# Norm factors of the second token half multiplied into its input blocks, and the query and output-operand splits moved to other turns, in a one-core attention layer

## The chip, the core and the metric

The kernel runs on one core of one Trainium2 chip. The metric is the device time of one execution in microseconds (us). The engines are named as the profile names them: PE (TensorE; its weight loads stand apart as PEld), DVE (VectorE), ACT (ScalarE), POOL (GpSimd) and SP (SyncE, whose queue issues nearly all DMAs here). Every engine works through its own instructions in order; tiles written by one and read by another are guarded by semaphores, so an instruction that waits holds up all that stand behind it on its engine.

## The reference

One encoder layer on x of 2048 tokens by 1024 channels, tokens lying on a grid of 32 rows by 64 columns:

```
h = rmsnorm(x, norm_0)                         # x * rsqrt(mean(x*x)) * norm_0
q, k, v, gate = split(h @ w_in_0, 4)           # w_in_0: 1024 x 4096; 16 heads of 64
o = neighbourhood_attention(q, k, v, rpb_0)    # each token sees a window of 8 rows x 16 columns,
                                               # with a learned bias, softmax in float32
x = x + (o * silu(gate)) @ w_out_0
return rmsnorm(x, norm_f)
```

The norm has two factors: `norm_0`, one per channel, and 1/rms, one per token. `h @ w` can take the second either before the product (in h) or after it (on the result's tokens), since a factor per token passes through the product. The change is about that choice.

## The kernel before, in words

**Precision.** Matrix products are made of three products of split operands: each operand t is split into a high part h (ACT copies it into the fp32r type) and the rest l = t - h (DVE subtracts), and PE adds h·h, h·l and l·h. A split therefore costs one ACT and one DVE instruction of 128x512.

**Layout.** Inputs stand transposed, channels on partitions and 512 tokens to a block; c = 0, 1, 2, 3 numbers the blocks of tokens. Tokens 0 to 1023 (c = 0, 1) are the first half, the rest (c = 2, 3) the second.

**Stage one** (`stage_one`, to 326 us): for the first half, the values v of all heads (`values_of`), and then q, k and gate with Strassen-Winograd's seven products instead of eight (`seven_products`): a unit is one kind (k, q, g) of one pair of heads j, 12 units in all, 7 x 12 matmuls each. After each product DVE adds the bank to an earlier one (`add`, `out_`, L432, L438), and where a result is complete it is multiplied by `rb[c]`, the tokens' 1/rms spread over all partitions: by POOL (L439) or, for product 2, by DVE out of PSUM (`evac`, L326 and L328). `give` then splits a k, or makes SiLU of a gate (ACT tanh L340, DVE L341), and a DMA stores it 12 matmuls later.

**The norm.** `stats` makes 1/rms from sums of squares, `diagonal` puts it on a diagonal and splits that, and `spread_rstd` lets PE multiply it with ones, so that ACT can copy `rb[c]` out of a bank. Only `norm_0` is applied to inputs: `split_to` and `split_x` scale by `g0` while they split (L498, L499, L155, L156). Values take 1/rms as ACT's scale when they leave PSUM (`evac_v`, L377).

**Stage two** (`stage_two`, 326 to 471 us): the same for the second half with one pair of heads j = 0 (three units of seven products) and all values. The other heads' q, k, gate of the second half (`projections`) are 36 plain groups of 24 matmuls (L365 to L369), which fill PE's time between attention turns.

**Attention** (the last loop, 471 to 1043 us): 64 turns, two for each pair of heads and block of 8 grid rows; a turn has two column blocks. Turn i is one iteration: `begin` issues loads and, on even turns, POOL's tables of bias plus mask (`bias`, L945, up to six additions `em`); `feed` puts about 22 matmuls of projections, later of the output projection (`outputs`, L1223 to L1227), on PE; `middle` splits the queries (`split_q`, L498 and L499, tiles `qh`, `ql`); then comes PE's attention block: transposes of turn i-2's weights (`turns`, L986, copied out by DVE L1011 and ACT L1010 as `pta`), scores of turn i (`scores`, L963, then L970 on DVE and the exponential L973 on ACT), and values of turn i-2 (`values`, L1031, tile `o`). `normalise` has POOL scale the weights (L981) by DVE's reciprocal (L979). All of it takes turns in eight PSUM banks handed out in order: a bank is used again eight allocations later, when its readers are done.

**The order** of instructions is fixed by hand. A clock counts filling matmuls; `store` puts DMAs and other late work into a list with a lag on that clock; `feed` keeps at least 8 matmuls between the last split or evacuation and the attention block. Output operands are split by `split_og` (ACT L1103, DVE L1104, two halves) when `ahead` in `outputs` finds the next one loaded 28 matmuls ago. Loads of keys (L896), queries (L900), values (L920) and gates (L927) are issued by SP in the order of the list; `later_loads` spaces them.

Of the kernel before, what the change touches and what calls it, by code (L numbers as in the profile page):

```python
# [70 lines left out]
def build(ctx, tc, x, xr, xt, wg, rpb, w_out, n0, nf, masks, out):  # L71
# [65 lines left out]
    rb = {}  # L137
# [14 lines left out]
    def split_x(a, b, t, tiles=None):  # L152
        h, l = tiles or (xs([128, 512], F32R, "hh"), xs([128, 512], F32R, "hl"))
        hh[a, b], hl[a, b] = h, l
        nc.scalar.activation(h, t, AF.Copy, scale=g0[:, a:a + 1])  # L155
        nc.vector.scalar_tensor_tensor(l, t, g0[:, a:a + 1], h.bitcast(F32), op0=OP.mult, op1=OP.subtract)  # L156

    def use_item(it):
# [3 lines left out]
        if kind == "x":  # L162
            split_x(a, b, t, (hh[a, b], hl[a, b]))
# [125 lines left out]
    pending = []  # L289
# [23 lines left out]
    def flush(c):  # L313
        if c not in rb:
            if c not in dgs:
                diagonal(c)
            spread_rstd(c)
        for e in [e for e in pending if e[0] == c]:
            pending.remove(e)
            e[1]()  # L320

    def evac(kind, hp, c, p, then=None):
        state["event"] = clock[0]
        tmp = ev([128, 512], F32, "tmp")
        if kind == "k":
            nc.vector.tensor_tensor(tmp, p, rb[c], OP.mult)  # L326
        else:
            nc.vector.tensor_tensor(blocked(tmp), tiled(p), tiled(rb[c]), OP.mult)  # L328
# [5 lines left out]
    def give(kind, hp, c, tmp):  # L334
        while sum(e[1][0] in "kqg" for e in later) > 1:
            later.pop(0)[2]()
        s = slice(c * 512, c * 512 + 512)
        if kind == "g":
            sg = ev([128, 512], F32, "sg")
            nc.scalar.activation(sg, tmp, AF.Tanh, scale=0.5)  # L340
            nc.vector.scalar_tensor_tensor(sg, sg, 1.0, tmp, op0=OP.add, op1=OP.mult)  # L341
            written.add(("g", hp, c))
            store(("g", hp, c), 12, lambda: nc.sync.dma_start(sgd[hp][:, s], sg))
            return
        written.add((kind, hp, c))
        if kind == "q":
            store(("q", hp, c), 12, lambda: nc.sync.dma_start(qd[hp][:, s], tmp))
            return
        hi = ev([128, 512], F32R, "hi")
        lo = ev([128, 512], F32R, "lo")  # L350
        nc.scalar.activation(hi, tmp, AF.Copy)
        nc.vector.tensor_tensor(lo, tmp, hi.bitcast(F32), OP.subtract)
# [22 lines left out]
    def evac_v(u, t, p):  # L375
        v = ev([128, 512], F32, "v")
        nc.scalar.activation(v, p, AF.Copy, scale=rt[:, t:t + 1])  # L377
# [10 lines left out]
    def seven_products(us, c0, X1, also):  # L388
# [45 lines left out]
        def out_(n, a, c, P, u, then):  # L434
            kind, j = us[n]
            tmp = ev([128, 512], F32, "tmp")
            lay, of = (lambda t: t, lambda t: t) if kind == "k" else (blocked, tiled)
            nc.vector.tensor_tensor(lay(tmp), of(B[n, P]), of(u), OP.add)  # L438
            nc.gpsimd.tensor_tensor(lay(tmp), lay(tmp), of(rb[c]), OP.mult)  # L439
# [16 lines left out]
        def run():  # L456
            then = []
            for i, (n, P) in enumerate(seq):
# [7 lines left out]
                elif P == 2:  # L466
                    evac(kind, 2 * j, c0, B[n, 2], then)
# [74 lines left out]
    def stage_one():  # L542
# [31 lines left out]
        def also(n, i):  # L574
# [10 lines left out]
            if (n, i) == (-1, 3):  # L585
                spot2 = mkp([128, 3, 512], F32, "spot")
                L2["x11"] = [spot2[:, k] for k in range(3)] + [lp([128, 512], F32, "land")]
                for k in range(4):
                    load_x(2, "x11", k, L2["x11"][k])
            if n == 0:  # L590
                if i == 0:
# [3 lines left out]
                    for k in (0, 1):  # L595
                        split_to(*X2["B11"][k], L2["x11"][k], gain("x11", k))
                elif i == 1:
                    L2["x21"] = [p([128, 512], F32, "land") for p in (mp, mp, ep, ep)]
                    for k in range(4):
                        load_x(2, "x21", k, L2["x21"][k])  # L600
                    for a, b in ((1, 1), (0, 2), (1, 2)):
                        load_v0(0, a, b)
                    for k in (2, 3):
                        split_to(*X2["B11"][k], L2["x11"][k], gain("x11", k))
# [12 lines left out]
                elif i in (4, 5):  # L617
                    for k in (0, 1) if i == 4 else (2, 3):
                        split_to(*X2["B21"][k], L2["x21"][k], gain("x21", k))
# [3 lines left out]

        ahead, run = seven_products(us, 0, X1, also)
# [113 lines left out]
    def stage_two():  # L738
        x12, x11, x21 = L2["x12"], L2["x11"], L2["x21"]
        x22 = [qp([128, 512], F32, "land") for _ in range(4)]  # L740
        for k in range(4):
# [3 lines left out]
                 "T4": [(vp, 512)] * 4 + [(mp, 512)] * 2 + [(ep, 512), (qp, 512)]}  # L745
# [49 lines left out]
        def t123(*ks):  # L795
            def g():
                for k in ks:
                    y = ev([128, 512], F32, "y")
                    a, b, c = x11[k], x12[k], x22[k]
                    nc.scalar.activation(y, b, AF.Copy, scale=gain("x12", k))  # L800
                    nc.vector.tensor_tensor(b, b, a, OP.subtract)
                    nc.vector.scalar_tensor_tensor(c, c, gain("x22", k), y, op0=OP.mult, op1=OP.subtract)
# [566 lines left out]
```

## Time and profile before

| | |
|---|---|
| median of 3 runs | 1101.96 us (1101.08 to 1102.29) |
| profiled execution | 1102.79 us |
| its span, first to last instruction | 1101.0 us |
| busy, share of the span | PE 98%, PEld 80%, DVE 67%, ACT 48%, POOL 34% |
| mean granted TensorE clock | 0.990 |
| DMA | 217.29 MB, mean 197 GB/s |

A row of a group says line, engine, operation, out<-in and shape, how many, busy time in all, the mean of one in ns, and the engine's idle time just before with what ended it. A row of a window has from:to, its length, and the busy time of each engine, then the granted clock, the share of the DMA engines and GB/s. In a timeline, a row has the start, the length, the engine, the line and what it does; brackets hold idle time before it and what ended it. PE counts as busy through a matmul's modelled end, so consecutive matmuls of 128x512 last 390 ns each and still start every 227 ns.

### The profile page before, as it was taken

What the parts mean: (1) busy time and instruction counts of PE and PEld (TensorE: products, weight loads), DVE (VectorE), ACT (ScalarE), POOL (GpSimd) and SP (SyncE); (2) the same over time, 40 slices, a digit from 0 to 9 for tenths busy, and PEclk for the clock granted to TensorE, in tenths of its full rate; (3) what the DMA queues carried; (4) which work ended last, traced back from release to release, by engine and by line L of the source; (5) the groups of instructions that cost most, each with busy time, mean ns of one, the idle gap of its engine ahead of it and who ended that gap; (6) DMA issues with size and microseconds to landing.
All of it is one profiled execution on the core that took longest, in us unless ns stands there. A gap on an engine that the chain in (4) does not pass through costs nothing.

```text
span 1101.0 us, 22543 instructions
## 1 busy us (share of the span) xinstructions
PE 1080.7 (98%) x7657; PEld 883.6 (80%) x7657; DVE 732.7 (67%) x1663; ACT 531.5 (48%) x1336; POOL 378.5 (34%) x483
## 2 busy tenths in 40 slices
PE   9999999999999999999999999999999999999997
PEld 6888888888888888877888888888877888887885
DVE  5376778788777337575665766665777777776644
ACT  7545343343344433255554554564556555555422
POOL 0000312222130001245445444424447666675200
PEclk9999999999999999998999999999999999999999
DMA  8633545454574235587767878687979797887452
GB/s 307 209 96 105 185 132 181 143 173 112 166 216 138 80 89 157 195 263 232 233 193 241 251 223 230 211 268 222 259 237 286 228 288 225 252 274 211 152 153 77
DMA packets 142962, 217.29 MB, mean 197 GB/s; under 512 B 18048, under 2 KB 65408, under 8 KB 142848
## 3 DMA queue, kind: packets, MB, share of 16 engines
q1 hardware_dynamic: 142704, 215.58, 64.6%
q8 instruction: 62, 1.02, 0.4%
q14 instruction: 52, 0.43, 0.1%
q10 hardware_dynamic: 144, 0.26, 0.1%
HBM read 157.05 MB, written 58.72 MB: 196 GB/s over the span
## 4 chain that ended last, share of the span: by engine, by line
PE 88%; DVE 5%; DMA 3%; issue 2%; ACT 1%; POOL 1%; SPq 0%; DVEq 0%; POOLq 0%
PE pp L421 24%; PE pv L534 16%; PE o L1031 7%; PE s L963 6%; PE pp L369 6%; PE pp L367 6%; PE pp L365 5%; PE po L1227 5%; PE po L1223 4%; PE po L1225 4%; PE ph L986 4%; ACT x L973 1%; PE zp L1242 1%; DVE gl L1104 1%; DMA sgt<-sgd 0%
## 5 line engine op out<-in xcount | busy, mean ns | idle before, releaser
L981 POOL TENSOR_SCALAR x<-x,st 128x360 f32<-128x360 f32 (+5 forms) x256 | 143.1, 579 | 239.1 <-DVE st L979 157.1
L439 POOL TENSOR_TENSOR tmp<-tmp,rb 128x512 f32<-128x512 f32 x45 | 73.5, 1634 | 399.2 <-DVE tmp L438 358.4
L973 ACT ACTIVATE x<-x,st 128x360 f32<-128x360 f32 (+5 forms) x256 | 151.8, 594 | 56.4 <-DVE st L970 56.4
L421 PE MATMUL pp<-h,f 128*128 128x512 f32 x480 | 155.4, 389 | 0.0
L945 POOL TENSOR_TENSOR em<-e,mk 128x480 f32<-128x480 f32 (+5 forms) x160 | 140.8, 915 | 5.0 <-DVE st L970 5.0
L421 PE MATMUL pp<-t,f 128*128 128x512 f32 x540 | 129.8, 389 | 0.1
L970 DVE CUSTOM_DVE_ANT_0 x<-s,em 128x360 f32<-128x360 f32 (+5 forms) x256 | 123.8, 538 | 5.1 <-PE s L963 2.0
L421 PEld LDWEIGHTS pp<-t,f 128*128 128x128 f32 x540 | 101.3, 188 | 21.5 <-DVE u L432 0.6
L369 PE MATMUL pp<-h,w 128*128 128x512 f32 x288 | 115.9, 403 | 0.0
L367 PE MATMUL pp<-l,w 128*128 128x512 f32 x288 | 114.2, 397 | 0.0
L365 PE MATMUL pp<-h,w 128*128 128x512 f32 x288 | 113.6, 394 | 0.0
L1010 ACT ACTIVATE pta<-ph 96x256 f32<-96x256 f32 (+1 forms) x224 | 58.8, 333 | 105.8 <-PE ph L986 105.8
L1031 PEld LDWEIGHTS o<-pta,vt 96*64 96x64 f32 (+2 forms) x1792 | 86.0, 139 | 24.2 <-DVE pta L1011 10.2
L421 PEld LDWEIGHTS pp<-h,f 128*128 128x128 f32 x480 | 90.1, 188 | 18.8
L1031 PE MATMUL o<-pta,vt 96*64 96x128 f32 (+4 forms) x1792 | 95.2, 258 | 7.5 <-DVE pta L1011 4.6
L1227 PE MATMUL po<-wol,gh 128*128 128x512 f32 x252 | 101.4, 403 | 0.0
L1223 PE MATMUL po<-woh,gh 128*128 128x512 f32 x252 | 100.0, 397 | 0.0
L1225 PE MATMUL po<-woh,gl 128*128 128x512 f32 x252 | 99.7, 395 | 0.0
L1011 DVE COPY pta<-ph 128x384 f32<-128x384 f32 (+3 forms) x128 | 60.5, 513 | 51.5 <-PE ph L986 51.2
L421 PE MATMUL pp<-l,f 128*128 128x512 f32 x240 | 93.4, 389 | 0.0
L534 PE MATMUL pv<-wh,h 128*128 128x512 f32 x256 | 88.1, 390 | 0.0
L534 PE MATMUL pv<-wh,l 128*128 128x512 f32 x256 | 88.0, 389 | 0.0
(136 smaller groups left out, 1951.1 us busy)
## 6 DMA issues: line engine op xcount, KB each, us to landing
raw<-in_wg_dram SPq DMA_DIRECT2D x126, 256.0 KB
e<-in_rpb_dram SPq DMA_DIRECT2D x54, 240.0 KB
vt<-vd SPq DMA_DIRECT2D x256, 48.0 KB
row<-in_xr_dram SPq DMA_DIRECT2D x32, 256.0 KB
vd<-v SPq DMA_DIRECT2D x32, 256.0 KB
k_hi<-hi SPq DMA_DIRECT2D x32, 256.0 KB
k_lo<-lo SPq DMA_DIRECT2D x32, 256.0 KB
qd<-tmp SPq DMA_DIRECT2D x32, 256.0 KB
```

The source lines that it names most:

```text
L365: nc.tensor.matmul(p, wh[w, b][:, cols], hh[k, c], start=(k == 0), stop=False)
L367: nc.tensor.matmul(p, wh[w, b][:, cols], hl[k, c], start=False, stop=False)
L369: nc.tensor.matmul(p, wl[w, b][:, cols], hh[k, c], start=False, stop=(k == NK - 1))
L421: nc.tensor.matmul(B[n, P], t[:, int(m == 2), c], x[k][int(m == 1)], start=P in (1, 6, 5) and k == 0 and m == 0, stop=k == 3 and m == 2, s ...
L534: nc.tensor.matmul(ps[t], a[:, o], b, start=k == 0 and m == 0, stop=k == NK - 1 and m == 2)
L945: (nc.gpsimd if attending[0] or not s else nc.vector).tensor_tensor(sh(t), E[p, s][:, u0 + 4:u1 + 4, v0 + 8:v1 + 8], sh(MK[0][:, m0:m0 + n ...
L973: nc.scalar.activation(X[i, C][s], X[i, C][s], AF.Exp, bias=st[:, s:s + 1], scale=-1.0, accum_out=st[:, 2 + s:3 + s])
L981: nc.gpsimd.tensor_scalar(X[i, C][s], X[i, C][s], st[:, 4 + s:5 + s], 0.5, op0=OP.mult, op1=OP.mult)
L1031: nc.tensor.matmul(o[s * 64:s * 64 + 64, C * 128 + q0:C * 128 + q0 + nq], vt[C][:k, g - g0_, s * 64:s * 64 + 64], t[:k, at:at + nq], start ...
L1223: nc.tensor.matmul(p, gh, woh[q, j], start=(i == 0), stop=False)
L1225: nc.tensor.matmul(p, gl, woh[q, j], start=False, stop=False)
L1227: nc.tensor.matmul(p, gh, wol[q, j], start=False, stop=(i == NK - 1))
```

## The change

For the second half, 1/rms goes into the input blocks: `normed` multiplies a loaded block by `norm_0` and `rb[c]` in one DVE instruction, before it is split, and nothing is multiplied on the way out. So k, q and gate of the second half are given straight from PSUM (`give` with `psum`), sums of blocks need no gains, and `evac_v` takes 1.0 as its scale for t >= 8. For this `rb[2]` and `rb[3]` are made earlier, and the blocks x11 and x21 are loaded and normed in the last units of stage one. A gate is stored in its own token order, and the product with it (L1045 before) reads it in the other layout.

In attention, `split_q` for the next pair of heads moves from even turns to the odd turn before; query loads go into a pool of one buffer, one turn before their split; value loads come first in a turn, and keys, tables and gates later. `split_og` may run two places ahead in odd turns, and in even turns only for the place at hand or, from the fifth step of a group, the next.

```
@@ use_item
-            split_x(a, b, t, (hh[a, b], hl[a, b]))
+            normed("x%d1" % (a // 4 + 1), b, a % 4, t)
+            split_to(hh[a, b], hl[a, b], t, None)
@@ give
+    def give(kind, hp, c, t, psum=False):
...
         if kind == "g":
             sg = ev([128, 512], F32, "sg")
+            nc.scalar.activation(sg, t, AF.Tanh, scale=0.5)
+            nc.vector.scalar_tensor_tensor(sg, sg, 1.0, t, op0=OP.add, op1=OP.mult)
...
         if kind == "q":
+            if psum:
+                o = ev([128, 512], F32, "q")
+                nc.scalar.activation(blocked(o), tiled(t), AF.Copy)
+                t = o
...
+        nc.scalar.activation(hi, t, AF.Copy)
+        nc.vector.tensor_tensor(lo, t, hi.bitcast(F32), OP.subtract)
@@ out_, in seven_products
-            nc.gpsimd.tensor_tensor(lay(tmp), lay(tmp), of(rb[c]), OP.mult)
+            if c0 == 0:
+                nc.gpsimd.tensor_tensor(lay(tmp), lay(tmp), of(rb[c]), OP.mult)
@@ new
+    def normed(f, c, k, t):
+        nc.vector.scalar_tensor_tensor(t, t, gain(f, k), rb[c], op0=OP.mult, op1=OP.mult)
@@ also, in stage_one (n counts units from the last, i products of a unit)
+            if (n, i) == (-3, 1):
+                diagonal(2)
+            if (n, i) == (-3, 3):
+                spread_rstd(2)
+            if (n, i) in norms:
+                f, k = norms[n, i]
+                normed(f, 2, k, L2[f][k])
+            if (n, i) == (-3, 4):
+                diagonal(3)
...
+        norms = {(-2, 3): ("x11", 0), (-2, 5): ("x11", 1), (-1, 0): ("x11", 2), (-1, 1): ("x11", 3),
+                 (-1, 3): ("x21", 0), (-1, 4): ("x21", 1), (-1, 5): ("x21", 2), (-1, 6): ("x21", 3)}
@@ block, in stage_two
-                    split_to(*X2[f][k], x[k], gain(f, k))
+                    normed(f, 3, k, x[k])
+                    split_to(*X2[f][k], x[k], None)
@@ projections
-                pending.append((c, lambda kind=kind, hp=2 * j + a, c=c, p=p: evac(kind, hp, c, p)))
-                flush(c)
+                state["event"] = clock[0]
+                give(kind, 2 * j + a, c, p, True)
@@ load_qk
-            QT[p, T] = t = qp([128, 512], F32, "qr")
+            QT[p, T] = t = lp([128, 512], F32, "qr")
@@ ahead, in outputs
-            if n < ready["loaded"] and place[n] <= k + 1 and clock[0] - loaded_at[n] >= 28 and whole(n):
+            near = 2 if quiet[0] else 1 if i >= 4 else 0
+            if n < ready["loaded"] and place[n] <= k + near and clock[0] - loaded_at[n] >= 28 and whole(n):
@@ begin
+        if 0 < i <= N:
+            p, T, cs = pairs[i - 1]
+            later_loads(load_v(p, T, cs[0]) + load_v(p, T, cs[1]), 0, 1.25)
...
-                later_loads([kh, kl], 0, 2)
                 if nx[0] != p:
-                    later_loads(load_e(nx[0]), 4, 2)
-        if 0 < i <= N:
-            p, T, cs = pairs[i - 1]
-            later_loads(load_v(p, T, cs[0]) + load_v(p, T, cs[1]), 1, 1.5)
+                    later_loads(load_e(nx[0]), 6, 2)
+                later_loads([kh, kl], 10, 3)
+                NEXT.append(q)
...
-            later_loads([lambda: load_sg(p, T)], 7, 0)
+            later_loads([lambda: load_sg(p, T)], 15, 0)
@@ middle
-        if i % 2 or i >= N:
-            return
         m = i // 2
-        if type(QT[order[m]]) is not tuple:
-            split_q(*order[m])
-        if m + 1 < len(order):
-            later_loads([LOADS[m + 1][1]], 1, 0)
+        if i % 2 and m + 1 < len(order):
+            split_q(*order[m + 1])
+        elif i % 2 == 0 and NEXT:
+            later_loads([NEXT.pop()], 0, 0)
@@ the last loop
-        feed(a * 0.45)
+        feed(a * 0.25)
+        quiet[0] = i % 2 == 1 or i >= N
+        feed(a * 0.2)
         middle(i)
         feed(a * 0.55, 8)
+        quiet[0] = i >= N
```

More of the change, by code (lines that the diff above doesn't have):

```diff
@@ L466, in run @@
                 elif P == 2:
-                    evac(kind, 2 * j, c0, B[n, 2], then)
+                    if c0 == 0:
+                        evac(kind, 2 * j, c0, B[n, 2], then)
+                    else:
+                        then.append(lambda kind=kind, j=j, p=B[n, 2]: give(kind, 2 * j, c0, p, True))
                 elif P == 7:
@@ L589, in also @@
                     load_x(2, "x11", k, L2["x11"][k])
+            if (n, i) == (-2, 2):
+                L2["x21"] = [xp([128, 512], F32, "land") for _ in range(4)]
+                for k in range(4):
+                    load_x(2, "x21", k, L2["x21"][k])
+            if (n, i) in norms:
[3 more added lines that the diff above has]
+                diagonal(3)
             if n == 0:
@@ L595, in also @@
                     for k in (0, 1):
-                        split_to(*X2["B11"][k], L2["x11"][k], gain("x11", k))
+                        split_to(*X2["B11"][k], L2["x11"][k], None)
                 elif i == 1:
-                    L2["x21"] = [p([128, 512], F32, "land") for p in (mp, mp, ep, ep)]
-                    for k in range(4):
-                        load_x(2, "x21", k, L2["x21"][k])
                     for a, b in ((1, 1), (0, 2), (1, 2)):
@@ L808, in g @@
                 for k in ks:
-                    d = x21[k]
-                    nc.vector.scalar_tensor_tensor(d, d, gain("x21", k), x11[k], op0=OP.mult, op1=OP.subtract)
+                    nc.vector.tensor_tensor(x21[k], x21[k], x11[k], OP.subtract)
             return g
@@ L1110, in build @@
     squared = [0]
+    quiet = [False]
     def add_rows(n, j, ps):
@@ L1189, in more_rows, with ahead @@
             ready["res"] += 1
-        def ahead(k):
+        def ahead(k, i=0):
             n = ready["loaded"]
@@ L1228, in outputs @@
                 yield 1
-                ahead(k)
+                ahead(k, i)
             while k >= ready["res"]:
```

61 lines of the change are left out of this document (19 added, 42 removed).

## The prediction

> **What bounds the kernel now.** I read the windows by stage first, then the attention blocks in the chain of waits, then the timelines of the places where PE fell behind.
>
> ```profile
> core 0: us, PE busy (x) PEld busy (x) DVE busy (x) ACT busy (x) POOL busy (x), PEclk, DMA share, GB/s
> ...
> 97.56:326.28 228.72, 228.59 (x1009) 188.96 (x1008) 180.97 (x263) 87.71 (x168) 57.01 (x35) 1.00 0.52 161
> ...
> 414.49:471.40 56.91, 56.91 (x252) 47.13 (x252) 40.02 (x55) 18.75 (x33) 13.87 (x10) 1.00 0.55 180
> 471.40:495.90 24.50, 22.78 (x131) 17.66 (x130) 17.48 (x38) 11.78 (x29) 10.31 (x13) 1.00 0.84 264
> 495.90:1043.00 547.10, 538.12 (x5232) 439.49 (x5231) 368.24 (x1055) 300.28 (x896) 287.95 (x415) 0.98 0.79 237
> ```
>
> PE sets the time. The twelve units of stage one are 1008 matmuls in 228.7 us, one every 227 ns, with 0.1 us idle; stage two's units have no idle time at all. Nothing that is taken off DVE or POOL there can shorten anything. What can be won lies in attention: 1.7 us idle in its first turns, 9.0 us in the rest, and a clock of 0.98, which over 547 us is 11 us' worth of cycles if PE wants them all.
>
> ```profile
> 849.98 0.84 PE ph L986 x23
> 850.83 1.29 PE s L963 x11
> 852.11 1.49 PE o L1031 x32
> ...
> 927.86 0.74 PE ph L986 x17
> 928.71 1.09 PE s L963 x10
> 929.80 1.25 PE o L1031 x24
> ```
>
> These are attention blocks that wait for nothing: 3.62 us with the larger tables of grid rows, 3.19 us with the smaller. Against them stand four places:
>
> ```profile
> 492.10:500.80 8.70, 5.72 (x57) 4.38 (x56) 6.84 (x18) 4.98 (x17) 7.53 (x11) 0.72 0.90 270
> 500.80:504.20 3.40, 3.40 (x12) 2.48 (x10) 0.17 (x1) 0.58 (x3) 3.14 (x6) 0.71 0.76 249
> 807.50:813.30 5.80, 3.75 (x69) 3.07 (x68) 5.80 (x12) 1.98 (x7) 4.98 (x7) 1.00 0.91 250
> 813.30:822.80 9.50, 9.50 (x38) 7.47 (x34) 6.98 (x14) 6.59 (x17) 0.55 (x2) 0.82 0.79 252
> 829.30:835.60 6.30, 4.52 (x70) 3.96 (x69) 6.30 (x14) 2.60 (x10) 5.20 (x7) 0.86 1.04 334
> 835.60:841.30 5.70, 5.70 (x23) 4.45 (x21) 2.98 (x8) 3.50 (x9) 0.07 (x1) 0.85 0.86 255
> 1006.60:1011.70 5.10, 3.46 (x57) 3.07 (x56) 2.82 (x10) 3.54 (x11) 4.98 (x8) 0.97 0.64 190
> 1011.70:1017.90 6.20, 6.20 (x23) 4.75 (x21) 2.21 (x5) 0.77 (x3) 2.86 (x5) 0.75 0.56 151
> ```
>
> First the block, then the matmuls behind it. Each block is 2 to 5.5 us too long, and after each the granted clock is down. I price the clock at (1 - clock) times the stretch.
>
> **Why PE waits there.** At 807 us:
>
> ```profile
> 804.24 6.39 POOL L945 TENSOR_TENSOR em<-e,mk 128x360 f32<-128x360 f32 x6
> ...
> 806.91 1.72 DVE L499 SCALAR_TENSOR_TENSOR ql<-qr,qh 128x512 fp32r<-128x512 f32 x1 [1.13 <-ACT qh L498]
> ...
> 808.55 2.63 DVE L1104 TENSOR_TENSOR gl<-ograw,gh 128x512 fp32r<-128x512 f32 x2
> ...
> 811.83 1.56 PE L1031 MATMUL o<-pta,vt 96*64 96x128 f32 x32 [2.04 <-DVE pta L1011]
> ```
>
> It is an even turn, and POOL adds its six tables. Three DVE splits, each reading two tiles of SBUF, lie in that time and take 1.72 and 2.63 us; the copy `pta` stands behind them on DVE, and PE waits for it. The groups say what such splits cost on average, and what else the change touches:
>
> ```profile
> L439 POOL TENSOR_TENSOR tmp<-tmp,rb 128x512 f32<-128x512 f32 x45 | 73.5, 1634 | 399.2 <-DVE tmp L438 358.4 <-DMA raw<-in_wg_dram 12.9 <-DMA qr<-qd 12.0
> ...
> L499 DVE SCALAR_TENSOR_TENSOR ql<-qr,qh 128x512 fp32r<-128x512 f32 x32 | 30.4, 949 | 20.7 <-ACT qh L498 19.7 <-DMA vt<-vd 1.0
> ...
> L1104 DVE TENSOR_TENSOR gl<-ograw,gh 128x512 fp32r<-128x512 f32 x30 | 27.1, 939 | 2.1 <-ACT gh L1103 1.2 <-DMA vt<-vd 0.9
> ...
> L499 DVE SCALAR_TENSOR_TENSOR l<-land,g,h 128x512 fp32r<-128x512 f32 x34 | 26.1, 809 | 19.1 <-ACT h L498 19.1
> ...
> L328 DVE TENSOR_TENSOR tmp<-pp,rb 128x512 f32<-128x512 f32 x34 | 23.4, 689 | 37.1 <-PE pp L369 31.2 <-PE pp L421 5.8
> ```
>
> A DVE instruction of this size is 689 ns when one input is in PSUM; `ql` and `gl` average 949 and 939.
>
> **The change part by part.**
>
> *Norm factors, first two stages.* They add 20 multiplies (8 in stage one's last three units, 8 blocks and 4 reloaded blocks in stage two and its end), nearest row `l<-land,g,h`: 809 ns, so 16 us of DVE; and they remove nine POOL multiplies (1634 ns, 15 us) and three evacuations. PE covers all of it: DVE has 181.0 of 228.7 us in stage one, that is 15.1 of 19.1 us a unit, and six multiplies at 809 ns put 4.9 us into the fullest unit, one more than its free 4.0 us. The excess of 1 us falls into the next unit's free time, and DVE's results are needed a product (2.7 us) later at the earliest. I count 0; the bounds are 0 and 2 us. The two spreads of 1/rms are moved, not added.
>
> *Evacuation in projections.* 36 groups lose a DVE multiply (689 ns) from the way between PE's bank and its release. A key's bank is now held until ACT's `hi` and DVE's `lo` have read it, a query's until one ACT copy. DVE sheds 25 us; ACT gets 12 copies, 8 us at DVE's 689 ns, for which it has room (300 of 547 us). The gate's reordered product is not shown; the multiply at L328 read in that layout at 689 ns, so I count 0.
>
> *First turns.* This is where the evacuation counts:
>
> ```profile
> 491.74 5.67 POOL L945 TENSOR_TENSOR em<-e,mk 128x264 f32<-128x264 f32 x6
> ...
> 493.55 1.33 DVE L178 TENSOR_TENSOR w<-raw,w 128x512 fp32r<-128x512 f32 x1
> ...
> 494.80 0.68 DVE L326 TENSOR_TENSOR tmp<-pp,rb 128x512 f32<-128x512 f32 x1
> ...
> 495.54 0.43 PE L963 MATMUL s<-kt,qh 64*128 64x352 f32 x1 [1.47 <-DVE tmp L326]
> ```
>
> PE waits for the bank that `tmp` releases; ahead of it stand `ql` and a split that POOL's tables hold up. The loss is 8.70 - 3.19 = 5.5 us, and 0.29 x 3.4 = 1.0 us of clock. After the change `ql` is a turn earlier, `lo` reads PSUM and the ACT half needs no DVE first; the split `w` stays, and stays blocked. I keep 2.0 us of loss: **-4.5**.
>
> *Query and output splits.* At 807 us the loss is 5.80 - 3.62 = 2.2 and 0.18 x 9.5 = 1.7 us. In the changed kernel's order `ql` is gone from this turn, both `gl` are still in it. Without 1.7 us on DVE, 0.6 us of wait remain and, I take it, a full clock: **-3.3**. At 829 us (6.30 - 3.62 = 2.7, and 0.15 x 5.7 = 0.9 us) all three splits have left the turn: **-3.6**.
>
> *Loads.* At 1006 us another thing is late:
>
> ```profile
> 995.96 1.56 SPq L896 DMA_DIRECT2D kt<-k_hi  x1
> ...
> 1003.68 0.38 SPq L920 DMA_DIRECT2D vt<-vd  x1
> ...
> 1010.88 0.92 PE L1031 MATMUL o<-pta,vt 96*64 96x128 f32 x12 [1.64 <-DMA vt<-vd]
> ```
>
> SP is held 1.56 us with a key load, and the last value load is issued after keys, tables and gate, 3 us before its use. The change puts the eight value loads first. Loss 5.10 - 3.19 = 1.9 and 0.25 x 6.2 = 1.6 us: **-3.5**. Keys go out about 2.3 us later (10 matmuls), with two turns to go.
>
> *Smaller waits of even turns.*
>
> ```profile
> PE o L1031 <- DVE pta L1011: 4.6, 5, 2.0
> ```
>
> ```profile
> PEld o L1031 <- DVE pta L1011: 10.2, 16, 2.5
> ```
>
> Beyond the two long ones there are between 4.6 - 2 x 2.0 = 0.6 us (PE's own row) and 10.2 - 2 x 2.5 = 5.2 us (its weight loads', some of it hidden behind running scores) in up to 14 places. I take the middle, **-2.5**.
>
> *What the moved splits do.* Odd turns get one `ql` each and most `gl` pairs; the fullest, by the new order, has four `gl` halves, a `ql` and an addition. An odd turn has none of POOL's tables. DVE's average turn is 368.2 / 64 = 5.8 us now, in 22 x 0.227 + 3.6 = 8.6 us; with these five splits at 0.7 us, less what an odd turn loses, the fullest comes to some 8 us. Bounds: 0, and 1 us in each of the five turns that get two or more; I take **+1.4**.
>
> Sum: -4.5 - 3.3 - 3.6 - 3.5 - 2.5 + 1.4 = -16.0 us. The profiled execution was 1102.79 us (span 1101.0), so 1086.8; the median of the runs shown is 0.8 us lower: **1086 us**.
>
> The clock terms rest on one reading: a wait of 2.04 us at 811.83 is followed by a clock of 0.82 over the next stretch. [...]
>
> **The rivals.**
>
> *The waits move to the odd turns* (chance 0.18). POOL's scalings there block DVE as the tables do, and four `gl` ahead of `pta` cost what three splits cost at 807 us: 3.9 us with its clock. If three of the five loaded turns do so, 11.7 us come back instead of 1.4: about 1096 us. For it: DVE stays the engine behind `pta`. Against it: odd turns lack the 6.39 us of tables that the even one at 804 us has.
>
> *The query is late* (0.10, slower). A query is now asked for one turn ahead, not two, into a single buffer, and ACT must split it in the middle of the next turn; behind `qh` on ACT stand the evacuations and the copies `pta`, and PE waits for their banks.
>
> ```profile
> 462.57 3.85 DMA qr<-qd
> ```
>
> ```profile
> e<-in_rpb_dram SPq DMA_DIRECT2D x54, 240.0 KB
> vt<-vd SPq DMA_DIRECT2D x256, 48.0 KB
> ```
>
> With quiet queues it lands in 3.85 us; it has 8.6 us. Ahead of it now stand eight value loads and often two tables, up to 0.9 MB, 4 us at the 237 GB/s of attention. So it decides when the queue adds another 1 us of backlog at the issue. If each of 31 queries is 1 us late, the 16 us are spent and 15 more are lost: 1117 us. Against it: the share of the DMA engines is 0.79, and no ACT wait for `qr` appears now.
>
> *POOL's multiplies block the norm multiplies* (0.05). In stage one's last units c = 0 and 1 still go through POOL. If each of six multiplies waits a full 1.63 us, DVE overruns the two units by 1 + 9.8 - 4 = 7 us, and PE with it: 1093 us. [...] Against it: only three of seven products bring a POOL multiply.
>
> *It does nothing* (0.03): the splits wait for other things in their new places, 1102 us.
>
> **How the numbers follow.** The forecast has 0.64. Low end: all losses go, 6.5 + 3.9 + 3.6 + 3.5 + 5.2 = 22.7 us, 1079 us. High end: the first rival and 2 us for stage one, 1098 us. What is left out is the late query, no effect, and the tails, below 0.2. Faster by over 0.2% (2.2 us, about what a measurement here can tell): 0.86; within: 0.03; slower: 0.11.
>
> **What would show it.** Right: blocks at the old 807, 829 and 1006 within 1 us of 3.6 and 3.2 us, `ql` and `gl` near 0.7 us, a clock of 1.00 through attention but for its first turns, PE's idle time there under 4 us. Wrong: ACT waiting for `qr`; `o` waiting for `pta` in odd turns; any idle time of PE before 471 us.

## The result, and the profile after

The changed kernel takes 1117.52 us (median of four runs, 1116.2 to 1119.7) against 1101.62 us for the kernel before. The ratio is 1.0146, with a 95% interval of 1.0128 to 1.0164: **slower by 1.5%**, where 1086 us was forecast. The profiled execution took 1119.7 us, its span is 1117.5 us.

Where the 16.5 us lie is seen when the span is cut at the start of three attention blocks (the first `ph` of turns 3, 36 and 62, read off PE's timeline). First the kernel before, then the one after; columns as in the windows above: stretch, length, busy time of PE, PEld, DVE, ACT, POOL, clock, DMA share, GB/s.

```profile
504.20:792.00 287.80, 287.39 (x2802) 234.56 (x2803) 181.53 (x510) 153.22 (x466) 132.92 (x198) 1.00 0.78 231
792.00:1017.90 225.90, 218.90 (x2154) 179.17 (x2153) 166.86 (x478) 131.71 (x384) 140.88 (x193) 0.98 0.83 252
```

```profile
498.40:792.50 294.10, 289.77 (x2800) 236.36 (x2799) 159.28 (x483) 158.48 (x477) 135.26 (x205) 0.99 0.79 231
792.50:1034.40 241.90, 224.93 (x2153) 182.59 (x2152) 156.79 (x473) 131.11 (x384) 136.13 (x192) 0.96 0.80 234
```

Up to turn 3 the change gains 5.8 us (504.2 to 498.4). It gives back 6.3 us up to turn 36 and 16.0 us up to turn 62; the rest is 83.1 us in both. In the last stretch PE has 17.0 us of idle time instead of 7.0, at a clock of 0.96, and the same loads move at 234 GB/s instead of 252.

What was forecast of DVE and of the even turns is there. The groups of the changed kernel show `ql` at 692 ns and `gl` at 707 (949 and 939 before). The two places below, from PE's timeline, are the old 807 and 829 us; their blocks (here and below: from the first `ph` to the first filling matmul behind the block) are now 3.89 and 3.61 us instead of 5.81 and 6.24:

```profile
L494 DVE SCALAR_TENSOR_TENSOR ql<-qr,qh 128x512 fp32r<-128x512 f32 x32 | 22.1, 692 | 73.1 <-ACT qh L493 71.5 <-DMA vt<-vd 1.6
L1108 DVE TENSOR_TENSOR gl<-ograw,gh 128x512 fp32r<-128x512 f32 (+1 forms) x32 | 21.3, 707 | 9.9 <-ACT gh L1107 9.9
L493 ACT ACTIVATE qh<-qr 128x512 fp32r<-128x512 f32 x32 | 20.0, 624 | 48.1 <-DMA qr<-qd 48.1
```

```profile
810.48 1.56 PE L1035 MATMUL o<-pta,vt 96*64 96x128 f32 x32 [0.21 <-DMA vt<-vd]
...
828.07 1.56 PE L1035 MATMUL o<-pta,vt 96*64 96x128 f32 x32
```

The third row of the groups is the new thing: ACT's split of the query, which never waited in attention before, waits 48.1 us for `qr`. Turn 51 shows what that does (timeline of the changed kernel, rows of SP, ACT, DVE and PE):

```profile
928.28 0.34 SPq L904 DMA_DIRECT2D qr<-qd  x1
...
932.19 7.35 SPq L924 DMA_DIRECT2D vt<-vd  x8
933.99 0.63 ACT L493 ACTIVATE qh<-qr 128x512 fp32r<-128x512 f32 x1 [5.28 <-DMA qr<-qd]
...
934.65 0.69 DVE L494 SCALAR_TENSOR_TENSOR ql<-qr,qh 128x512 fp32r<-128x512 f32 x1 [5.14 <-ACT qh L493]
935.26 0.75 DVE L1170 SCALAR_TENSOR_TENSOR y<-y,st,acc 128x512 f32<-128x512 f32 x1
...
935.92 0.68 DVE L1140 TENSOR_TENSOR y<-po,xr 128x512 f32<-128x512 f32 x1
...
936.66 1.00 PE L967 MATMUL s<-kt,qh 64*128 64x384 f32 x3 [5.00 <-DVE y L1140]
```

SP issues the query at 928.28 us, though its place in the order is the middle of the turn before (about 919 us). It lands after 5.7 us (a landing is the last completion event on a DMA's semaphore before the next DMA there is issued). ACT waits for it 5.28 us, DVE behind ACT 5.14, and the output tile's addition `y`, which has nothing to do with the query, stands behind `ql`; PE waits 5.00 us for the bank that `y` releases. The window 930.5 to 941 us has a clock of 0.67. The block takes 10.50 us instead of 3.20. Twelve of the 31 odd turns with a split have long blocks, from 4.05 us up, where 3.0 to 3.6 us are usual. In all twelve ACT waits for `qr`, 0.87 us or more; in turn 49 PE itself waits for values as well, 1.11 us.

One more wait is new. A gate is now loaded at lag 15, and DVE's first work of a turn, `og`, reads it (waits of the changed kernel):

```profile
ACT qh L493 <- DMA qr<-qd: 48.1, 16, 6.2
...
DVE og L1049 <- DMA sgt<-sgd: 10.7, 5, 4.5
```

### The profile page after: what moved, and what is told of

It reads as the page before. It is cut to its first block, busy times and chain, and to the rows that moved or that the text cites. A ratio compares the mean times of both kernels' runs of the same rounds, so it can differ in the third digit from the quotient of the medians.

```text
span 1117.5 us, 22480 instructions
## 1 busy us (share of the span) xinstructions
PE 1085.1 (97%) x7657; PEld 886.2 (79%) x7657; DVE 702.6 (63%) x1644; ACT 531.0 (48%) x1345; POOL 357.2 (32%) x474
## 4 chain that ended last, share of the span: by engine, by line
PE 78%; DMA 8%; DVE 5%; SPq 3%; issue 2%; POOL 2%; ACT 2%; DVEq 0%; POOLq 0%; ACTq 0%
PE pp L409 23%; PE pv L529 16%; PE o L1035 6%; PE pp L357 5%; PE s L967 5%; PE pp L355 5%; PE pp L353 5%; PE po L1233 4%; PE po L1229 3%; PE po L1231 3%; PE ph L990 3%; DMA qr<-qd 2%; DMA kt<-k_lo 2%; DMA xr<-in_x_dram 2%; SPq L924 2%
## 5 line engine op out<-in xcount | busy, mean ns | idle before, releaser
L949 POOL TENSOR_TENSOR em<-e,mk 128x480 f32<-128x480 f32 (+5 forms) x160 | 135.9, 883 | 135.0 <-DMA mk<-in_masks_dram 132.2
L428 POOL TENSOR_TENSOR tmp<-tmp,rb 128x512 f32<-128x512 f32 x36 | 58.8, 1632 | 270.5 <-DVE tmp L426 231.8
L967 PE MATMUL s<-kt,qh 64*128 64x480 f32 (+5 forms) x512 | 85.2, 372 | 18.0 <-DVE y L1140 7.3
```

The costliest lines, as they stand in the source:

```text
L949: (nc.gpsimd if attending[0] or not s else nc.vector).tensor_tensor(sh(t), E[p, s][:, u0 + 4:u1 + 4, v0 + 8:v1 + 8], sh(MK[0][:, m0:m0 + n ...
L967: nc.tensor.matmul(pst[s], qq[a, qs], kk[a, :r1 - r0, c0:c1], start=(m == 0), stop=(m == 2))
```

## The experiments

Each ratio is against runs of the kernel before on the same chip, with its 95% interval. "To turn 3", "3 to 36" and "36 to 62" are the stretches above, read in the same way in the profiled execution: 504.2, 287.8 and 225.9 us before; 498.4, 294.1 and 241.9 us after.

### Is it the query?

**e1**, the query first in the even turn:

```
 def begin(i):
+        if i % 2 == 0 and i < N and m + 1 < len(order):
+            kh, q, kl = load_qk(*order[m + 1])
+            later_loads([q], 0, 0)
         if 0 < i <= N: ...            # values
 def middle(i):
-        elif i % 2 == 0 and NEXT:
-            later_loads([NEXT.pop()], 0, 0)
```

> The changed kernel, but the next query's load is asked for at the start of the even turn, ahead of the eight value loads, tables and keys, into the same single buffer; all else as changed. Theory L (the query lands late, and every long block of an odd turn, 33 us over their usual 3.1 and 3.55 us, and their low clock come from it): ACT's waits for qr fall from 48 us to under 10, the blocks of turns 43, 51 and 55 go from 9.0, 10.5 and 8.9 to under 4.5 us, and the time is 1083 to 1092 us. Rival O (odd turns now hold too much for DVE: the query split, four halves of output operands, an addition, evacuations that read PSUM): the query comes early, yet the blocks stay over 5 us and the time stays over 1105 us.

Measured: 1.0018 (0.9987 to 1.0049). 3 to 36 is 286.7 us, all of the loss there is gone; 36 to 62 is 233.2 us, more than half of it. ACT's waits for the query fall from 48.1 to 9.5 us:

```profile
ACT qh L493 <- DMA qr<-qd: 9.5, 9, 3.3
...
DVE og L1049 <- DMA sgt<-sgd: 39.4, 15, 4.6
```

So a query asked for ahead of the values wins 1.3%. But now DVE waits 39.4 us for gates, and values land up to 5.3 us after their block began. Neither theory stands alone.

**e2**, the query issued by ACT:

```
-            nc.sync.dma_start(t, qd[p][:, T * 512:T * 512 + 512])
+            (nc.scalar if attending[0] else nc.sync).dma_start(t, qd[p][:, T * 512:T * 512 + 512])
```

> The changed kernel, but in attention the query's load is issued by ACT instead of SP, at the same place in the order. Theory L1 (the query is late because it stands in SP's queue behind value, table and key loads, of which only eight may be under way; once issued it lands in about 4 us): asked in the middle of the even turn, it is there a turn later, and the time is 1083 to 1095 us. Theory L2 (the 16 DMA engines are what is late, with 0.9 MB ahead of it): the lead stays short, and the time stays over 1110 us. Rival O: over 1105 us too, but with ACT's waits for qr gone.

Measured: 1.0113 (1.0065 to 1.016). 36 to 62 takes 242.2 us, with new long blocks in turns 38 and 40 (9.05 and 9.22 us). In the traces of the kernel before and of the changed one all 1184 DMAs take eight completion semaphores in turn, whichever engine issues them (ACT issues one), and never more than eight are under way. In turn 38 a value load of SP has the semaphore of ACT's query; that lands at 808.46 us, and the load goes out at 808.53 (timeline):

```profile
802.03 0.33 ACTq L904 DMA_DIRECT2D qr<-qd  x1
804.64 0.34 SPq L335 DMA_DIRECT2D qd<-q  x1
808.53 1.23 SPq L924 DMA_DIRECT2D vt<-vd  x3
```

The second queue was no way around SP's here, so this run does not tell L1 from L2.

**e3**, the kernel before with a late query and nothing else:

```
 def middle(i):
+        if i % 2:
+            if NEXT: later_loads([NEXT.pop()], 0, 0)
+            return
...
-            later_loads([LOADS[m + 1][1]], 1, 0)
+            NEXT.append(LOADS[m + 1][1])
```

> The kernel before, but each query is loaded one turn ahead of its split (in the middle of the odd turn, behind that turn's value loads) instead of two; the split stays in the even turn, and nothing of the change is in it. Theory L: a lead of one turn is too short whatever else is changed; ACT waits for qr in most even turns, and the time goes up by 5 to 25 us, 1107 to 1127 us. If the late query needs the change's own load order (tables, keys and gate between the value loads and the query), an odd turn with only value loads ahead of it is quick enough: 1100 to 1105 us. Rival O expects no change: 1102 us.

Measured: 1.0035 (1.0011 to 1.006), 19.1 us of ACT waits in 7 turns. A lead of one turn costs 4 us even there, between the two ranges that were given.

**e4**, the norm factors alone (the loop of attention, `near` and the query's pool as before):

> Only the part of the change that moves the norm factors (blocks multiplied by rb on the way in, k, q and gate given straight from PSUM, the reordered gate product), with the load order, the splits in even turns and the lead of two turns of the kernel before. Theory L: nothing of the loss is here; the first turns gain 4 to 6 us and PE has no idle time before 471 us: 1094 to 1099 us. Rival N (ACT's copies of queries and DVE's reads of PSUM hold banks longer and cost PE waits all through the projections): over 1105 us.

Measured: 0.9959 (0.9931 to 0.9987); 499.1, 286.3 and 229.6 us. This part does what was forecast: 5.1 us are won up to turn 3 and 1.5 up to turn 36. By turn 62 it has given back 3.7.

### The steps one by one

Three edits are combined here. "Old order" of loads is that of the kernel before:

```
 def begin(i):
-        if 0 < i <= N: later_loads(load_v(...) + load_v(...), 0, 1.25)     # values, first
...
+                later_loads([kh, kl], 0, 2)                                # was 10, 3
+                later_loads(load_e(nx[0]), 4, 2)                           # was 6, 2
+        if 0 < i <= N: later_loads(load_v(...) + load_v(...), 1, 1.5)
+            later_loads([lambda: load_sg(p, T)], 7, 0)                     # was 15
```

"Two turns ahead" is a query asked for right behind the split of the one before, which frees the single buffer:

```
         if i % 2 and m + 1 < len(order):
             split_q(*order[m + 1])
+            if m + 2 < len(order):
+                later_loads([load_qk(*order[m + 2])[1]], 1, 0)
```

And the split of the query may go back to the even turn, its load into the four-buffer pool.

**e5**, changed kernel, two turns ahead, old order:

> The changed kernel with the query asked for right after the split of the one before (two turns ahead, same single buffer), and with the load order of the kernel before: keys first, then values, tables, gate. Splits stay in odd turns. Theory L+V (both losses are loads: the query one turn ahead, and the big loads bunched behind the values, so that the next turn's values come late): no ACT wait for qr over 1 us, the last value loads land within 1 us of the block's start, and the time is 1084 to 1094 us. Rival O (DVE in odd turns): over 1100 us with blocks of odd turns still over 4.5 us while qr and vt have landed.

Measured: 1.0011 (0.9989 to 1.0034). No wait for `qr`; 36 to 62 is down to 222.5 us, but 3 to 36 takes 291.4, of which turn 3 loses 4.9 us to values that land 6.5 us after its block began. (The profiled execution is 4.3 us faster than the median.)

**e6**, changed kernel, two turns ahead, changed order:

> The changed kernel with only the query asked for right after the split of the one before, two turns ahead; the load order stays as changed. Theory L+V: the query is never late, the values still are, as in the run with the query first (they landed up to 5 us after their block began): 1095 to 1106 us. Theory L alone (only the query's lead): 1084 to 1094 us.

Measured: 1.0095 (1.0067 to 1.0123), slower than either theory had it. ACT waits 0.4 us for queries, yet 36 to 62 takes 239.4 us, and DVE waits 36.7 us for gates. That e1, with the shorter lead, is 0.8% faster stays open: in e6 the query stands between the loads of the odd turn, in e1 ahead of them, which these runs do not separate.

**e7**, changed kernel, split in the even turn, changed order:

> The changed kernel with the query split back in the even turn and its load two turns ahead into the four-buffer pool, as before; norm factors, output-operand splits and load order stay as changed. Theory L+V: no query is late, but values still land late: 1095 to 1106 us, the even turns' ql again up to 1.8 us. If the order of loads costs nothing: near 1096 us, that is the norm part's 4 us (0.9959 of before) and some 3 us for the output-operand splits. Rival O (odd turns too full): under 1092 us, since the split has left them.

Measured: 1.006 (1.0043 to 1.0077); 284.9 and 239.3 us. **e15**, the same with the old order:

> Norm factors and output-operand splits as changed, query split and query load in even turns and two turns ahead as before, loads in the old order: e7 with nothing but the load order set back. If the changed order of loads costs by itself: 1093 to 1099 us against e7's 1107.8. If not: 1104 us or more.

Measured: 0.9968 (0.9945 to 0.999); 285.6 and 228.2 us. Between e7 and e15 only the load order differs. What waits in e7, and how it reaches PE in turn 54:

```profile
DVE og L1049 <- DMA sgt<-sgd: 35.3, 14, 5.8
...
POOL em L949 <- DMA e<-in_rpb_dram: 10.0, 9, 2.5
```

```profile
948.97 0.69 DVE L1049 TENSOR_TENSOR og<-o,sgt 128x512 f32<-128x512 f32 x1 [5.35 <-DMA sgt<-sgd]
950.95 0.63 ACT L1143 ACTIVATE xr<-y 128x512 f32<-128x512 f32 x1 [5.57 <-DVE y L1140]
951.58 0.61 ACT L493 ACTIVATE qh<-qr 128x512 fp32r<-128x512 f32 x1
...
952.24 0.85 PE L967 MATMUL s<-kt,qh 64*128 64x288 f32 x4 [3.45 <-ACT qh L493]
```

In e15 DVE has no wait for a gate at all, and POOL's for tables are 2.0 us. In e7 the gate is asked for at lag 15; DVE stood at `og`, all that stands behind it stood too, and PE waited for a query split whose data had landed at 942.5 us, 9 us before the split. That the gate's lag alone would do it was not tried.

**e8**, changed kernel, one turn ahead, old order:

> The changed kernel with only the load order set back to that of the kernel before (keys first, gate earlier); the query is still asked for one turn ahead into one buffer and split in the odd turn. Theory L: the query stays late, 1103 to 1115 us, ACT's waits for qr over 25 us in sum. Theory V alone (only the order is at fault): 1086 to 1096 us.

Measured: 1.0077 (1.0061 to 1.0094), with 43.1 us of ACT waits for `qr`. So the edits lie side by side, each step one edit:

| | ratio |
|---|---|
| norm factors (e4) | 0.9959 |
| and output splits moved (e15) | 0.9968 |
| and query split in odd turns, asked two turns ahead (e5) | 1.0011 |
| and the changed load order (e6) | 1.0095 |
| and the query one turn ahead, as changed | 1.0146 |

The other way round, from e5 to e8 to the changed kernel, the lead costs 0.66% and the order 0.69%. So the lead costs 0.5 to 0.7%, the order 0.7 to 0.8% (0.9% from e15 to e7). The moved output splits change nothing that the intervals show (e4 to e15). With the query split in odd turns 0.4% is lost (e15 to e5, whose intervals just touch).

**e16**, e5 with the first four turns in the changed order:

> e5 (odd-turn splits, query asked for two turns ahead, old load order) with the changed order, values first, in the first four turns only, where e5 lost 6 us (block of turn 3: 7.9 us, waiting for values that landed 6.5 us after its start). Expected: 1092 to 1098 us, faster than before and than the norm factors alone; over 1100 us if the first turns were not what e5 lost.

Measured: 1.0 (0.9986 to 1.0014); the expected gain did not come. Turn 3 still has a block of 5.68 us. Of the versions that leave the computation whole, e4 and e15 beat both kernels, by 0.3 to 0.4% against the one before.

### Are the DMA engines the limit?

**e9** to **e12** load the values of a column block in one DMA instead of four:

```
-        def rows(r):
-            if r == 0:
-                VT[p, T, C] = vp([128, 4, 128], F32, "vt")
-            nc.sync.dma_start(VT[p, T, C][r * w:r * w + w, :g1_ - g0_].rearrange("p g d -> p (g d)"), src[r])
+        def rows():
+            VT[p, T, C] = vp([128, 4, 128], F32, "vt")
+            nc.sync.dma_start(VT[p, T, C][:4 * w, :g1_ - g0_].rearrange("p g d -> p (g d)"), src)
```

> The changed kernel with two value loads a turn instead of eight: one DMA for the four rows of a column block, same bytes, same place in the order (lags 0 and 5). Theory S (SP's queue is the limit: each DMA on SP waits until the one issued eight before it has landed, and eight small value loads fill that window, so that the big loads and the query behind them are issued late): queries and values land 3 to 6 us earlier, and the time is 1086 to 1100 us. Theory B (the DMA engines cannot deliver the bytes in time): no change, 1110 to 1120 us.

> The run with the query two turns ahead and the old load order, with two value loads a turn instead of eight. Theory S: the late values of turns 40, 41, 59 and 61 go, 1084 to 1094 us. Theory B: 1097 to 1106 us, as without it.

> The kernel before with two value loads a turn instead of eight. Theory S: little is late there but turn 61's values, so 2 to 6 us are won: 1095 to 1100 us. Theory B: 1098 to 1104 us, not to be told from the kernel before.

> The run with the norm factors alone, with two value loads a turn instead of eight. Theory S: 1088 to 1096 us; what stays are the even turns in which ql and gl meet POOL's tables (turns 38 and 40). Theory B: 1095 to 1101 us, as without it.

Measured: 1.0318 (1.0286 to 1.0351), 1.039 (1.0361 to 1.0419), 1.0326 (1.0294 to 1.0358) and 1.0301 (1.027 to 1.0331). All four (the changed kernel, e5, the kernel before and e4 with that edit) are far slower, which neither theory said. In the large form the values landed after 9.5 us (median, 790 to 1030 us, changed kernel) instead of 4.2, and other loads became slower too (`qr` 8.2 instead of 4.9 us). The traces' completion events differ with it: in the kernel before each of 608 DMAs of 128 rows posts 16 and each of 256 value loads of 24 rows 13, and the large form posts 5 each time. Why it lands late was not shown. The four runs do not tell S from B.

**e13** takes bytes away, **e14** does so in e16, **e17** in the kernel before:

```
 def load_res(n, j):
-        nc.sync.dma_start(RES[n, j], x[...])
 def add_rows(n, j, ps):
-        nc.vector.tensor_tensor(y, ps, xr, OP.add)
+        nc.vector.tensor_tensor(y, ps, late["nf"][j], OP.add)
 def load_e(p, pool_=None):
+        if attending[0]: rows(0); E[p, 1] = E[p, 0]
```

> The changed kernel with fewer bytes loaded in attention: the output tiles add the final norm's vector, which is resident, instead of a loaded block of x (no such load at all, some 5.9 MB of 59 MB between 790 and 1030 us), and both heads of a pair use the first head's bias table, so that one table of 240 KB is loaded instead of two. That part of the computation is changed; the instructions of PE, DVE, ACT and POOL are the same. Theory B (the DMA engines are the limit in the last 30 turns, and lateness is bytes queued ahead): queries and values land earlier, 1090 to 1103 us. Theory P (the place in the order alone, with its one-turn lead): the time stays at 1108 us or more.

Measured: 0.9911 (0.9889 to 0.9933). The same order, and 26 us less:

```profile
498.40:785.90 287.50, 287.38 (x2802) 234.75 (x2801) 160.03 (x481) 159.00 (x477) 135.10 (x204) 1.00 0.76 224
785.90:1006.00 220.10, 216.80 (x2155) 176.08 (x2154) 158.28 (x476) 131.33 (x384) 137.04 (x192) 1.00 0.75 220
```

```profile
ACT qh L493 <- DMA qr<-qd: 21.2, 12, 3.4
DVE og L1054 <- DMA sgt<-sgd: 1.4, 2, 1.0
```

36 to 62 falls from 241.9 to 220.1 us at a full clock; gates are nearly in time. Queries are still late in 12 turns.

> The kernel of e16 (early query, old load order) with the same bytes taken away as in e13. Theory B: all late loads go and the gains of the prediction stand free: 1078 to 1088 us. Theory P: the order is already right, so nothing more to win: within 4 us of e16.

Measured: 0.9905 (0.9886 to 0.9924). The median, 1090.6 us, is above theory B's range, but with the bytes gone, lead and order make no difference to the time that the intervals show. ACT has no wait for `qr` here; the stretches are 498.8, 288.7 and 217.0 us.

> The kernel before with the same bytes taken away as in e13 (no block of x for the output tiles, one bias table for both heads of a pair; that part of the computation is changed). If the DMA limit cost the kernel before little, since its order met its deadlines: 1096 to 1101 us, so that the change, freed of late loads, is worth 5 to 10 us by e13's 1091.2. If fewer bytes help any kernel alike: under 1088 us, and the change is worth nothing or less even then.

Measured: 0.994 (0.991 to 0.9971); 503.9, 287.4 and 218.7 us. With most late loads gone, the change is worth 0.9911 / 0.994, that is 0.3% or 3 us, and since the two intervals overlap, even that is not certain. In the profiles e13 is 5.5 us ahead of e17 at turn 3 and loses 1.4 us of that between turns 36 and 62, where e14, with its queries in time, gains 1.7.

**e18** replaces the loads left out in e13 by loads of 32 columns into the same tiles:

> e13 with the number and the order of the transfers of the changed kernel: each load that e13 left out is replaced by one of 32 columns (16 KB instead of 240 or 256) into the same tile. That part of the computation is changed as in e13. Theory B (bytes through the DMA engines): as e13, 1088 to 1096 us. Theory S (slots: SP lets only eight transfers be under way, each for 4 to 5 us whatever its size, so the number of transfers is the limit): most of e13's gain is lost, 1102 to 1116 us. Between the two if small transfers hold a slot for half as long.

Measured: 0.993 (0.9907 to 0.9952), against 0.9911 for e13. Of the 2.35% that e13 won, 2.16% come from bytes at the same number of transfers. The small tables took as long from issue to landing as the full ones beside them (medians 3.4 and 3.1 us, 790 to 1030 us), so nothing was won on their slots; the small blocks of x took 4.0 us (5.9 in the changed kernel). The median, 1097.4 us, lies above theory B's range, on a chip where the kernel before takes 1105.8; and the profile has 290.5 and 224.7 us, with long blocks in turns 5, 44 and 55, so a part for the number of transfers is not excluded. In the main theory B holds: bytes are what makes the loads late. Whether the DMA engines or something else on the bytes' way sets the rate was not tried.

## Why the prediction was wrong, point by point

Two costs were put at nothing, the later loads and the query's shorter lead; together they are 1.35% (e5 to the changed kernel), some 15 us. And of the 16.0 us that were forecast as won, only those of the first turns stayed: with lead and order of loads as before the time is 1.0011 of the kernel before (e5), and with the query's split in even turns too 0.9968 (e15).

*What bounds the kernel.* Wrong for the last 30 turns. The idle time there was read wait by wait, as DVE's, with a DMA share of 0.79 put down as "against" the rival. But between turns 36 and 62 the loads run at 252 GB/s, with 6.6 of 8 transfers under way on average (the times from issue to last completion of all that were issued between 790 and 1030 us, over 240 us), and 15% fewer bytes (220 GB/s over 218.7 us in e17, 252 over 225.9 before) shorten even the kernel before by 0.6%. A mean share of 0.8 was no reserve, though it is no ceiling either: the prediction's own window at 829.30 us has a share of 1.04 and 334 GB/s. Loads come in bursts, and a mean over 550 us does not show whether one is late.

*First turns, -4.5.* Right: the start of turn 3 moves from 504.2 to 498.4 us, 5.8 us with 0.5 us from earlier stages. In turn 2 `s` now waits for `lo`, 0.59 us where it waited 1.47 us for `tmp`, and the block falls from 8.75 to 4.29 us (timeline of the changed kernel):

```profile
493.48 0.67 PE L967 MATMUL s<-kt,qh 64*128 64x352 f32 x4 [0.59 <-DVE lo L340]
```

*Old 807 and 829 us, -3.3 and -3.6.* The mechanism is right, and the blocks are within 0.3 us of 3.6, as was asked for. As forecast `gl` is still slow at 807 (2.22 us for two beside POOL's tables), and the wait is 0.21 us instead of 2.04.

*The clock term.* It rested on one reading, and that reading does not repeat. With fewer bytes the kernel before has the same block with the same wait, and the clock after it stays full:

```profile
811.17 1.56 PE L1036 MATMUL o<-pta,vt 96*64 96x128 f32 x32 [2.04 <-DVE pta L1016]
```

```profile
812.70:820.00 7.30, 7.30 (x34) 6.06 (x33) 6.12 (x13) 6.27 (x15) 0.49 (x1) 1.00 0.82 270
```

2.04 us were followed by 0.82 once and by 1.00 once. Three places were too few, and the sum without the three clock terms (1.7, 0.9 and 1.6 us), -11.8 us, should have had a chance of its own.

*Values at 1006 us, -3.5.* Failed. The block there is 6.03 us in the changed kernel (5.10 before). Its query landed 2.2 us after its start, and `s` waited 2.22 us. In e17 it is 3.09 us: fewer bytes mended it, and the change does not load fewer.

*Loads: "keys go out about 2.3 us later, with two turns to go", and no price for the gate.* **This is the first step that failed.** Loads that are asked for later were put at nothing, without working out when they land. The order itself costs 0.7 to 0.9%, 8 to 10 us (e8 to the changed kernel, e5 to e6, e15 to e7), and the query's shorter lead another 0.5 to 0.7%. The part names keys, not the gate, which moved from lag 7 to 15 and is read by `og`, the first DVE work of a later turn (35.3 us of waits in e7, none in e15).

*Smaller waits, -2.5, and moved splits, +1.4.* In e13, between turns 36 and 62, six even turns gain 5.6 us of block length against e17 (turn 38: 3.76 for 5.80; 40: 3.61 for 4.81; 56: 3.08 for 4.05). Without 38 and 40 that is 2.3 us, about the smaller waits as forecast. The others lose 6.6 us (44: 5.49 for 3.75; 51: 4.94 for 3.09; 58: 4.36 for 3.11). In turn 51 of e13 the query's split, a scaling and the addition are in one line on DVE, and `s` waits 0.92 us for its bank:

```profile
916.01 0.69 DVE L494 SCALAR_TENSOR_TENSOR ql<-qr,qh 128x512 fp32r<-128x512 f32 x1 [1.70 <-ACT qh L493]
916.62 0.75 DVE L1174 SCALAR_TENSOR_TENSOR y<-y,st,acc 128x512 f32<-128x512 f32 x1
917.28 0.68 DVE L1144 TENSOR_TENSOR y<-po,acc 128x512 f32<-128x512 f32 x1
...
918.02 0.62 PE L972 MATMUL s<-kt,qh 64*128 64x384 f32 x3 [0.92 <-DVE y L1144]
```

But ACT's split ahead of `ql` had waited 1.84 us for its query. In e14, where no query is late, the even turns gain the same, and the others lose 3.5 us, not 6.6 (51: 1.1; 44: 0.7; 58: nothing). So about half of the loss goes with late queries, and the moved splits cost at most 3.5 us in this stretch: more than +1.4, within its bounds. The first rival, that the waits move to the odd turns, has a small part and not its 11.7 us.

*The rival "the query is late".* Right in kind and, by luck, in size: 1117 us against 1117.5. Its working had 31 queries 1 us late each; there were 16 waits of 3 us on average, and the order cost as much again. It was given 0.10 on two grounds, both wrong. That no ACT wait for `qr` appeared before says nothing when the lead is what is changed: the time from the query's issue to `qh` was 6.4 to 22 us in the kernel before, and now it is 3.9 to 10.5. And one turn was counted from the place in the program; SP issued the query up to 9 us behind that place, since it stands behind value loads that wait for their buffers and for semaphores (from 498 to 1035 us the two largest sums of SP's waits at value loads are 27.9 us for the landing of `kt<-k_lo`, in 25 places, and 17.2 us for `o`, in 15).

*Norm multiplies in the first two stages, 0.* Right: between 97.5 and 330 us PE is busy for 232.15 us (232.37 before), so if POOL's multiplies block the new ones, PE does not see it; turn 0 starts at 478.3 us (478.8 before).

## What to carry to other kernels

A load that is asked for later or later in its queue is priced by when its queue issues it, not by when the program names it; list every load whose place or lag changes, and for each the first instruction that reads it and what stands behind that on its engine. Loads were late here at a mean DMA share of 0.80 (36 to 62, changed kernel) with 6.8 of 8 transfers under way; take bytes away in an experiment before you count idle time of PE as another engine's. A wait that is removed in a stretch that is short of bytes can be given back at a later load (e4: 3.7 of 6.6 us).

## What the runs showed of the hardware

With values loaded in the form that posts 5 completion events, every kind of load took 8 to 11 us to land in place of 3.5 to 6 (medians from 790 to 1030 us, e11 and the kernel before), and the kernel before lost 3.3%.

The clock after a wait is not set by its length alone: the 2.04 us above gave 0.82 and 1.00. In the kernel before the low clock behind the three waits comes in pieces of 3.41 us at half speed (windows 813.38 to 816.79, 833.86 to 837.27 and 1011.35 to 1014.77 us: 0.50 each), so each of the three waits cost 1.7 us of clock, wherever the windows of the prediction were cut; e17 has no such piece between 503.6 and 1090.6 us. What sets it beside the length of the wait was not shown.

Beside POOL's tables DVE instructions of a single column were slow as well. In e13's turn 44 the root of an output tile falls beside six tables, and four steps of the form SCALAR_TENSOR_TENSOR take 0.79 to 1.15 us each; the next, as the tables end, takes 0.16. Three TENSOR_SCALAR steps just before them, beside the tables too, take 0.15 to 0.20 and are not slowed (in the kernel before 0.15 to 0.22 both beside tables and apart from them; there SCALAR_TENSOR_TENSOR takes 0.61 to 1.80 beside them and 0.16 to 0.22 apart):

```profile
851.88 1.15 DVE L1163 SCALAR_TENSOR_TENSOR st<-st 128x1 f32<-128x1 f32 x1
853.07 1.02 DVE L1164 SCALAR_TENSOR_TENSOR st<-st 128x1 f32<-128x1 f32 x1
...
855.78 0.16 DVE L1167 SCALAR_TENSOR_TENSOR st<-st 128x1 f32<-128x1 f32 x1
```

```profile
850.25 5.48 POOL L954 TENSOR_TENSOR em<-e,mk 128x360 f32<-128x360 f32 x6
```
